# Hybrid decoder layer: keys and values projected between the recurrent branch's channels, queries last

## The chip, the cores and the metric

The kernel runs on one core of a Trainium2 chip. Its engines work side by side and wait for each other through semaphores: PE (matmul; its weight loads are listed as PEld), DVE (elementwise work and scans), ACT (activation functions, casts and copies), POOL (GpSimd) and SP (which here issues most DMAs). The metric is the device time of one execution in microseconds, as the median of the runs.

## The reference, cut to what matters

One decoder layer is computed for a prompt of 2048 tokens, with 16 meta tokens ahead of it, and for 64 sample tokens.

```python
hn = rmsnorm(x, g_mix_pre)
proj = hn @ w_in
q, k, v, xl, gate = jnp.split(proj, [512, 1024, 1536, 2048], axis=-1)
attn = attend(q, k, v)               # stick-breaking, 8 heads of 64
...
xc = conv_b; xc = xc + xpad[:, j:j + T] * conv_w[j]      # j = 0..3
r = sigmoid(xb @ w_gate_a + b_gate_a);  i = sigmoid(xb @ w_gate_x + b_gate_x)
log_a = -8 * softplus(-lru_lambda) * r
h = exp(log_a) * h + sqrt(-expm1(2 * log_a)) * i * xc    # scan over tokens
...
mixed = concat([attn, lru * gelu(gate)]) @ w_out
x = x + rmsnorm(mixed, g_mix_post)
u = relu(rmsnorm(x, g_mlp_pre) @ w_up)
x = x + rmsnorm((u * u) @ w_down, g_mlp_post)
```

In stick-breaking attention a logit block passes two sigmoids, a running product along the keys and a multiplication; the result is transposed and multiplied with the values. Keys, values, the last hidden state and the last convolution inputs are outputs too.

## The kernel before

**Tiles.** The prompt is worked in four tiles of 512 tokens (NSB = 4, index s); tile 0 also carries the meta and the sample tokens, 592 columns in two chunks. Matmuls run on float32 split into a high and a low part in the fp32r format, three products for each (high x high, high x low, low x high). `gemm` computes 128 output channels for all tokens of a tile: 24 matmuls of 512 columns. `gemm_nat` computes 128 tokens by 512 channels in up to four PSUM accumulators. PSUM buffers have three tags: D (4, projections), T (3, logits and transposes), O (1, attention outputs).

**Weights.** A list `seq` holds the weight tiles in the order of use. `w_next` hands out the next one, already split by ACT (L161) and DVE (L162), splits the one behind it and starts the load of the one after that (SP, L152). Two raw and two split buffers each exist.

**Order of work.** PE's order is the order of the program, written by hand. The other engines' order is made by a scheduler when the kernel is built, out of dependencies and its own clock, so an instruction of DVE, ACT, POOL or SP can stand ahead of one that the program has earlier.

**Input projection.** `inproj(s)` runs, for the four channel groups c of the recurrent branch, the x gemm, the convolution (DVE, L508 and L510) and the gate gemm with GeLU (L527 to L530). After the x gemm of group c+1 come the two small gate matmuls of group c (`gates`, L455) with their sigmoids; they are kept in `held` until then. After the x gemm of group 2 `recur((0, 1))` runs the recurrence of groups 0 and 1: tanh, exp and sqrt on ACT (L466, L467, L469), products and a scan on DVE (L472, L473, L481), the product with the gate (L486) and a store to a DRAM tile `md` (L487). Then come four key gemms, each with a cast and split (L545, L546) and stores to `kd`. The gates of group 3 follow the first of them and `recur((2, 3))` the second (`late`). Then comes the value product (`gemm_nat`, evacuated by `v_evac`, stores to `vd`), and last the generator `queries()` with four query gemms; in the last two the next tile is normalised (`prep`) and transposed into `ahi` and `alo` (L264 to L267).

**Attention as side work.** `Work` holds generators that emit attention: first that of the samples, then `attn`, over tiles, heads and key groups. A step of `attn` may hold a logit block S (L706, then `chain`: sigmoids L642 and L643, scan L647 or L650, product L654), a transpose T (L716, evacuated by L727 and L728; for the meta keys by L722 to L724) and a product with the values V (L738, L740); T follows S, and V follows T, by four steps or more. Each gemm calls `tick` with an estimate of its PE time; `tick` adds that times `rate` to a credit and takes steps while the credit lasts. `rate` is RATE0 in the recurrent groups and RATE1 in keys, values and queries (tiles 1 to 3; in tile 0 it is 0). `need(key)` takes steps at once, without matmuls of a projection between them, until that piece of work is done. A tile's attention can start when its `queries()` has ended.

**After the last projection.** For tile 3 one query gemm is run; then `work.need("s")`, the pool `p1` (the projection's buffers) is closed and the pool `pacc` is opened in its memory. `group(0)` calls `work.need(("a", 0))`. Two more query gemms run while `load` brings `md` of tile 0 through the x buffers of `pacc` (L970) and splits it (L966, L967); then come the output projection of tile 0, the last query gemm, a stage of attention and transposes without gemms (`burst`), and the MLP with the rest of the attention and of the output projections between its gemms.

Of the kernel before, what the change touches and what calls it, by code (L numbers as in the profile page):

```python
# [8 lines left out]
F32 = mybir.dt.float32  # L9
# [3 lines left out]
AF = mybir.ActivationFunctionType  # L13
ALU = mybir.AluOpType
PSUM = bass.MemoryType.PSUM

P = 128
# [6 lines left out]
DB = 8  # L24
DS = 8
# [4 lines left out]
G0 = 1.5957691216057308  # L30
G1 = 0.07135481627159986
# [56 lines left out]
def _program(tc, I, O, NSB, NSC):  # L88

    nc = tc.nc  # L90
# [39 lines left out]
    seq = []  # L130
    for s in range(NSB):
        for c in range(4):
            seq.append(I["w_in"][12 + c])
            seq.append(I["w_in"][16 + c])
        seq += [I["w_in"][ct] for ct in range(4, 8)] + [I["w_v"][kp] for kp in range(4)]
        if s < NSB - 1:
            seq += [I["w_in"][ct] for ct in range(4)]
    out_w = [I["w_out"][hf, kp] for hf in range(2) for kp in range(4)]
# [295 lines left out]
    def inproj(s, p1, pa, K, ahi, alo, before_k=None):  # L434
# [53 lines left out]
                if s == 0:  # L488
                    nc.sync.dma_start(msd[:, 4 + c, :], gt[:, NP:N])

        held = None
        for c in range(4):
            outs = gemm(hi_, lo_, chunks, before_k=before_k if c == 0 else None)
            if held is not None:
                gates(*held)
            if c == 2:
                recur((0, 1))
            xp = T(p1, [P, 3 + W], F32, "xp")
            if s == 0:
                nc.gpsimd.memset(xp[:, 0:3], 0.0)  # L500
            else:
                nc.scalar.copy(xp[:, 0:3], K["convc"][:, c, :])
            for (a, b), o in zip(chunks, outs):
                nc.scalar.copy(xp[:, 3 + a:3 + b], o)
            nc.scalar.copy(K["convc"][:, c, :], xp[:, NP:NP + 3])
            cw = K["cw"]
            xc = T(p1, [P, W], F32, "xc", 1)
            nc.vector.tensor_scalar(xc[:, 0:NP], xp[:, 0:NP], cw[:, c, 0:1], K["cb"][:, c:c + 1], op0=ALU.mult, op1=ALU.add)  # L508
            for j in range(1, 4):
                nc.vector.scalar_tensor_tensor(xc[:, 0:NP], xp[:, j:j + NP], cw[:, c, j:j + 1], xc[:, 0:NP],  # L510
                                               op0=ALU.mult, op1=ALU.add)
            if s == 0:
                spad = T(p1, [P, DB, DS + 3], F32, "spad", 2)
                nc.gpsimd.tensor_copy(spad[:, :, 0:3], K["sconv"][:, c])
                nc.gpsimd.tensor_copy(spad[:, :, 3:3 + DS], xp[:, 3 + NP:3 + N].rearrange("p (b t) -> p b t", b=DB))
                nc.gpsimd.tensor_copy(K["csamp"][:, c], spad[:, :, DS:DS + 3])
                xs = xc[:, NP:N].rearrange("p (b t) -> p b t", b=DB)
                nc.vector.tensor_scalar(xs, spad[:, :, 0:DS], cw[:, c, 0:1], K["cb"][:, c:c + 1], op0=ALU.mult, op1=ALU.add)
                for j in range(1, 4):
                    nc.vector.scalar_tensor_tensor(xs, spad[:, :, j:j + DS], cw[:, c, j:j + 1], xs, op0=ALU.mult, op1=ALU.add)  # L520
            outs = gemm(hi_, lo_, chunks)
            g = T(p1, [P, W], F32, "g")
            for (a, b), o in zip(chunks, outs):
                nc.scalar.copy(g[:, a:b], o)
            g = g[:, 0:N]
            gt = T(p1, [P, W], F32, "gt", 2)[:, 0:N]
            nc.vector.scalar_tensor_tensor(gt, g, G1, g, op0=ALU.mult, op1=ALU.mult)  # L527
            nc.vector.scalar_tensor_tensor(gt, gt, G0, g, op0=ALU.add, op1=ALU.mult)
            nc.scalar.activation(gt, gt, AF.Sigmoid)
            nc.vector.tensor_tensor(gt, gt, g, op=ALU.mult)  # L530
            gts.append(gt)
            held = (c, xc)

        late = lambda c: gates(*held) if c == 0 else recur((2, 3)) if c == 1 else None


        work.rate = RATE1 if s else 0.0
        for c in range(4):
            outs = gemm(hi_, lo_, chunks)
            late(c)  # L540
            kf, hi, lo = stage("sf", F32), stage("sh", F32R), stage("sl", F32R)
            for (a, b), o in zip(chunks, outs):
                nc.scalar.copy(kf[:, a:b], o)
# [16 lines left out]
        def v_evac(t, o):  # L560
# [19 lines left out]
            else:  # L580
# [4 lines left out]
        gemm_nat(lambda k, t: ahi[:, k, t * P:min(t * P + P, N)], lambda k, t: alo[:, k, t * P:min(t * P + P, N)],  # L585
                 5 if s == 0 else 4, None, v_evac)

        def queries():
            ys = None
            for c in range(4):  # L590
# [3 lines left out]
                if c == 3 and s + 1 < NSB:  # L594
                    def nxt(k):
                        if k > 0:
                            xpose_k(ys, k - 1, K["g_pre"], ahi[:, k - 1], alo[:, k - 1])
                outs = gemm(hi_, lo_, chunks, after_k=nxt)
                if nxt is not None:
                    nxt(KC)  # L600
                hi, lo = stage("sh", F32R), stage("sl", F32R)
# [583 lines left out]


    next(queries)
    work.need("s")
    close(p1)
    pacc = xpool[0] = pool("pacc")  # L1190
# [149 lines left out]
```

## Time and profile before

| What | Value |
| --- | --- |
| median of 3 runs | 2724.7 us (2722.91 to 2725.73) |
| profiled execution | 2732.83 us, span 2731.0 us |
| granted PE clock, mean | 0.992 |
| busy DVE, ACT, POOL | 67%, 53%, 13% |
| input projection of tile 3, without queries | 478 to 596 us |
| first query gemm of tile 3 | from 596 us |
| output projection of tile 0 | from 627 us |

A row of the timeline has the start, the duration, engine, line, operation, output and inputs, shapes, the count, and in brackets the engine's idle time before it and what ended it. A row of the list of waits has the total, the number of times and the longest. Matmuls are pipelined and their ends are modelled: the start of one to the start of the next tells what each costs.

### The profile page before, as it was taken

What the parts mean: (1) busy time and instruction counts of PE and PEld (TensorE: products, weight loads), DVE (VectorE), ACT (ScalarE), POOL (GpSimd) and SP (SyncE); (2) the same over time, 40 slices, a digit from 0 to 9 for tenths busy, and PEclk for the clock granted to TensorE, in tenths of its full rate; (3) what the DMA queues carried; (4) which work ended last, traced back from release to release, by engine and by line L of the source; (5) the groups of instructions that cost most, each with busy time, mean ns of one, the idle gap of its engine ahead of it and who ended that gap; (6) DMA issues with size and microseconds to landing.
All of it is one profiled execution on the core that took longest, in us unless ns stands there. A gap on an engine that the chain in (4) does not pass through costs nothing.

```text
span 2731.0 us, 36901 instructions
## 1 busy us (share of the span) xinstructions
PE 2672.5 (98%) x13804; PEld 2213.0 (81%) x13804; DVE 1839.0 (67%) x2898; ACT 1453.2 (53%) x2430; POOL 352.9 (13%) x579
## 2 busy tenths in 40 slices
PE   8999999999899999999999999999999999999997
PEld 7987768778688888878888888878888887898895
DVE  6556377876877777869777777786777746333344
ACT  6556376865666554546565555565555534332232
POOL 3122331111211101011100100110000001000002
PEclk9999999999899999999999999999999999999999
DMA  4466858485444433445343334443333244222223
GB/s 164 137 216 194 260 179 233 123 229 167 144 128 119 115 110 103 140 145 176 100 115 112 101 112 125 161 149 110 101 102 101 76 162 160 82 81 85 78 85 108
DMA packets 149155, 368.11 MB, mean 135 GB/s; under 512 B 20992, under 2 KB 51200, under 8 KB 148976
## 3 DMA queue, kind: packets, MB, share of 16 engines
q1 hardware_dynamic: 103792, 287.35, 32.3%
q0 software_dynamic: 45184, 78.41, 11.6%
q8 instruction: 109, 1.79, 0.3%
q14 instruction: 70, 0.57, 0.1%
HBM read 305.51 MB, written 60.04 MB: 134 GB/s over the span
## 4 chain that ended last, share of the span: by engine, by line
PE 88%; DVE 6%; issue 2%; DMA 1%; ACT 1%; POOL 1%; SPq 0%; POOLq 0%; DVEq 0%; ACTq 0%
PE D L184 13%; PE D L186 13%; PE D L185 13%; PE D L216 11%; PE D L217 11%; PE D L218 11%; PE T L716 5%; PE T L706 4%; PE O L738 2%; PE O L740 2%; PE D L455 1%; DVE wlo L162 1%; POOL rstd L240 1%; PE O L222 1%; PE O L221 1%
## 5 line engine op out<-in xcount | busy, mean ns | idle before, releaser
L162 DVE TENSOR_TENSOR wlo<-wraw,whi 128x1024 fp32r<-128x1024 f32 x368 | 453.1, 1231 | 453.7 <-ACT whi L161 443.4
L184 PE MATMUL D<-ahi,whi 128*128 128x512 f32 (+3 forms) x1920 | 709.3, 369 | 0.0
L186 PE MATMUL D<-ahi,wlo 128*128 128x512 f32 (+3 forms) x1920 | 685.6, 357 | 0.2 <-DVE wlo L162 0.2
L185 PE MATMUL D<-alo,whi 128*128 128x512 f32 (+3 forms) x1920 | 684.0, 356 | 1.3 <-DVE ms L236 1.3
L161 ACT CAST whi<-wraw 128x1024 fp32r<-128x1024 f32 x368 | 386.9, 1051 | 493.5 <-PE D L217 300.1
L216 PE MATMUL D<-whi,uh 128*128 128x512 f32 x1024 | 417.5, 408 | 5.1 <-DVE y L1020 4.9
L184 PEld LDWEIGHTS D<-ahi,whi 128*128 128x128 f32 x1920 | 364.5, 190 | 50.1 <-issue 7.3
L217 PE MATMUL D<-whi,ul 128*128 128x512 f32 x1024 | 405.0, 396 | 0.0
L186 PEld LDWEIGHTS D<-ahi,wlo 128*128 128x128 f32 x1920 | 364.3, 190 | 50.0 <-DVE wlo L162 0.6
L218 PE MATMUL D<-wlo,uh 128*128 128x512 f32 x1024 | 404.5, 395 | 0.0
L185 PEld LDWEIGHTS D<-alo,whi 128*128 128x128 f32 x1920 | 365.2, 190 | 42.7 <-issue 1.7
L642 ACT ACTIVATE keep<-T,nbias 128x512 f32<-128x512 f32 (+6 forms) x352 | 210.1, 597 | 250.1 <-PE T L706 242.4
L650 DVE TENSOR_TENSOR_SCAN pb<-keep,carry 128x513 f32<-128x513 f32 (+1 forms) x228 | 267.5, 1173 | 74.9 <-ACT keep L642 71.8
L728 DVE TENSOR_TENSOR wtl<-T,wth 128x512 fp32r<-128x512 f32 (+1 forms) x320 | 191.2, 602 | 83.8 <-ACT wth L727 83.3
L727 ACT CAST wth<-T 128x512 fp32r<-128x512 f32 (+1 forms) x320 | 166.6, 523 | 129.5 <-PE T L716 128.9
L216 PEld LDWEIGHTS D<-whi,uh 128*128 128x128 f32 x1024 | 192.8, 188 | 46.6 <-DVE y L1020 6.6
L218 PEld LDWEIGHTS D<-wlo,uh 128*128 128x128 f32 x1024 | 192.6, 188 | 46.6
L217 PEld LDWEIGHTS D<-whi,ul 128*128 128x128 f32 x1024 | 193.3, 189 | 38.7
L643 ACT ACTIVATE beta<-T,bias 128x512 f32<-128x512 f32 (+6 forms) x352 | 208.4, 592 | 0.0
L654 DVE TENSOR_TENSOR beta<-beta,pb 128x512 f32<-128x512 f32 (+7 forms) x360 | 202.8, 563 | 0.0
L716 PE MATMUL T<-ident,beta 128*128 128x128 f32 (+1 forms) x1216 | 193.1, 276 | 7.2 <-DVE ms L236 3.6
L706 PE MATMUL T<-kv,q 128*128 128x512 f32 (+5 forms) x640 | 178.5, 361 | 4.1 <-DVE alo L267 3.3
(235 smaller groups left out, 3472.1 us busy)
## 6 DMA issues: line engine op xcount, KB each, us to landing
wraw<-in_w_up SPq DMA_DIRECT2D x128, 512.0 KB
wraw<-in_w_down SPq DMA_DIRECT2D x128, 512.0 KB
wraw<-in_w_in SPq DMA_DIRECT2D x64, 512.0 KB
q<-qd POOLq DMA_DIRECT2D x64, 256.0 KB, 4.9
wraw<-in_w_out SPq DMA_DIRECT2D x32, 512.0 KB
kv<-kd POOLq DMA_DIRECT2D x48, 256.0 KB
kv<-vd POOLq DMA_DIRECT2D x48, 256.0 KB, 4.1
y<-in_x_prompt SPq DMA_DIRECT2D x16, 512.0 KB
```

Source lines behind the costliest of these rows:

```text
L161: nc.scalar.copy(hi, r)
L162: nc.vector.tensor_tensor(lo, r, hi.bitcast(F32), op=ALU.subtract)
L184: nc.tensor.matmul(o, whi[:, k, :], ahi(k, a, b), start=(k == 0), stop=False)
L185: nc.tensor.matmul(o, whi[:, k, :], alo(k, a, b), start=False, stop=False)
L186: nc.tensor.matmul(o, wlo[:, k, :], ahi(k, a, b), start=False, stop=(k == KC - 1))
L216: nc.tensor.matmul(o, h, whi[:, kk, :], start=st, stop=False)
L217: nc.tensor.matmul(o, l, whi[:, kk, :], start=False, stop=False)
L218: nc.tensor.matmul(o, h, wlo[:, kk, :], start=False, stop=sp)
L642: nc.scalar.activation(keep[:, o:512], S, AF.Sigmoid, bias=nbias, scale=-0.125)
L650: nc.vector.tensor_tensor_scan(pb[:, o:513][:, ::-1], kr, kr, 1.0 if carry is None else carry, op0=ALU.mult, op1=ALU.bypass)
L706: nc.tensor.matmul(o, H["q"][:, e, i * P:(i + 1) * P], kap, start=(e == 0), stop=(e == 1))
L716: nc.tensor.transpose(t[0:kn, i * P:(i + 1) * P], w[:, c0:c0 + kn], ident)
```

## The change

Keys and values move between the recurrent groups. The order in a tile is now: key gemm 0, values, x and gate gemm 0; key gemm 1, x and gate gemm 1; key gemm 2, x and gate gemm 2; x and gate gemm 3; key gemm 3; then the four query gemms. `held` becomes a list: the gates of a group are run after the next gemm that asks for them, now a key gemm for groups 0, 1 and 3 and the x gemm 3 for group 2. `recur((0, 1))` stays behind x gemm 2. `recur((2, 3))` moves behind the first query gemm. RATE0, which now holds for all but key gemm 3 and the queries, goes from 0.2 to 0.35; RATE1 stays 0.5. For tile 3 `lru_outputs` (the stores of the last state) moves behind the first query gemm.

```diff
 for s in range(NSB):
     for c in range(4):
-        seq.append(I["w_in"][12 + c])
-        seq.append(I["w_in"][16 + c])
-    seq += [I["w_in"][ct] for ct in range(4, 8)] + [I["w_v"][kp] for kp in range(4)]
+        seq += [I["w_in"][4 + c]] if c < 3 else []
+        seq += [I["w_v"][kp] for kp in range(4)] if c == 0 else []
+        seq += [I["w_in"][12 + c], I["w_in"][16 + c]]
+    seq.append(I["w_in"][7])
...
-        held = None
+        held = []
+        def keys_of(c):
+            outs = gemm(hi_, lo_, chunks, before_k=before_k if c == 0 else None)
+            if held:
+                gates(*held.pop())
...
+        def values():
+            gemm_nat(lambda k, t: ahi[:, k, t * P:min(t * P + P, N)], lambda k, t: alo[:, k, t * P:min(t * P + P, N)],
+                     5 if s == 0 else 4, None, v_evac)
         for c in range(4):
-            outs = gemm(hi_, lo_, chunks, before_k=before_k if c == 0 else None)
-            if held is not None:
-                gates(*held)
+            if c < 3:
+                keys_of(c)
+            if c == 0:
+                values()
+            outs = gemm(hi_, lo_, chunks)
+            if held:
+                gates(*held.pop())
             if c == 2:
                 recur((0, 1))
...
-            held = (c, xc)
-        late = lambda c: gates(*held) if c == 0 else recur((2, 3)) if c == 1 else None
+            held.append((c, xc))
         work.rate = RATE1 if s else 0.0
-        for c in range(4):
-            outs = gemm(hi_, lo_, chunks)
-            late(c)
...
+        keys_of(3)
...
                 outs = gemm(hi_, lo_, chunks, after_k=nxt)
+                if c == 0:
+                    recur((2, 3))
...
             for _ in queries:
                 pass
-        lru_outputs(s, K)
+            lru_outputs(s, K)
...
     next(queries)
+    lru_outputs(NSB - 1, K)
     work.need("s")
...
-RATE0, RATE1, RATE2, RATE3, RATE4, BURST = 0.2, 0.5, 0.5, 0.55, 0.3, 4.0
+RATE0, RATE1, RATE2, RATE3, RATE4, BURST = 0.35, 0.5, 0.5, 0.55, 0.3, 4.0
```

The bodies of `keys_of` and `values` (with `v_store` and `v_evac`) are those of the old loops, unchanged.

More of the change, by code (lines that the diff above doesn't have):

```diff
@@ L489, in recur @@
                     nc.sync.dma_start(msd[:, 4 + c, :], gt[:, NP:N])
-        held = None
-        for c in range(4):
+        held = []
+        def keys_of(c):
             outs = gemm(hi_, lo_, chunks, before_k=before_k if c == 0 else None)
-            if held is not None:
-                gates(*held)
[L496 to L520, printed above, removed]
-            outs = gemm(hi_, lo_, chunks)
[L522 to L531, printed above, removed]
-            held = (c, xc)
@@ L534, in inproj @@
-        late = lambda c: gates(*held) if c == 0 else recur((2, 3)) if c == 1 else None
-        work.rate = RATE1 if s else 0.0
-        for c in range(4):
-            outs = gemm(hi_, lo_, chunks)
-            late(c)
+            if held:
+                gates(*held.pop())
             kf, hi, lo = stage("sf", F32), stage("sh", F32R), stage("sl", F32R)
@@ L588, in queries @@
+        work.rate = RATE1 if s else 0.0
+        keys_of(3)
         def queries():
```

39 lines of the change are left out of this document (37 added, 2 removed).

## Prediction

> **What bounds the kernel now.** I read the page first (engine shares, chain of waits), then the waits of the matrix engine (PE), then busy time by stage, and last the timeline of the one stage that stands out.
>
> ```profile
> span 2731.0 us, 36901 instructions
> PE 2672.5 (98%) x13804; PEld 2213.0 (81%) x13804; DVE 1839.0 (67%) x2898; ACT 1453.2 (53%) x2430; POOL 352.9 (13%) x579
> PE 88%; DVE 6%; issue 2%; DMA 1%; ACT 1%; POOL 1%; SPq 0%; POOLq 0%; DVEq 0%; ACTq 0%
> ```
>
> PE is busy 98% of the span, and the chain of waits is PE for 88%. The change removes no matmul, so it can only remove PE's idle time, 2731.0 - 2672.5 = 58.5 us in all, and time at a reduced clock. Where is it? First PE's waits from 176 to 602 us, the input projections of tiles 1 to 3, which are what the change reorders:
>
> ```profile
> PE T L706 <- DVE alo L267: 0.6, 1, 0.6
> ...
> PE D L186 <- DVE wlo L162: 0.2, 1, 0.2
> ```
>
> These are the first and last of five rows, each of 0.2 to 0.6 us, about 1.7 us together. Then the stages (columns: length, busy time and instruction count of PE, weight loads, DVE, ACT, POOL, granted clock, DMA share, GB/s):
>
> ```profile
> 478.00:602.00 124.00, 123.33 (x585) 99.34 (x584) 98.97 (x177) 92.51 (x161) 19.64 (x40) 1.00 0.58 167
> 602.00:614.00 12.00, 6.06 (x26) 4.36 (x25) 10.34 (x19) 7.19 (x15) 2.16 (x4) 0.83 0.93 263
> 614.00:627.00 13.00, 13.00 (x54) 10.47 (x54) 7.74 (x10) 6.82 (x11) 0.00 (x0) 0.90 0.78 269
> 687.00:719.00 32.00, 19.49 (x95) 14.99 (x94) 29.89 (x57) 22.37 (x43) 7.71 (x14) 0.79 0.56 172
> ```
>
> Tile 3's projection (478 to 602) keeps PE full. Evening out DVE and ACT inside it can therefore win next to nothing. Two stages lose time: 602 to 614 (5.94 us idle) and 687 to 719 (12.5 us idle, but DVE is busy 29.89 of 32: bound by DVE, and the change moves none of its work). So the question is what becomes of 602 to 614.
>
> **The stage from 602 to 614.** PE's timeline:
>
> ```profile
> 602.33 0.39 PE L738 MATMUL O<-wth,kv 128*128 128x512 f32 x1
> ...
> 602.80 0.27 PE L716 MATMUL T<-ident,beta 128*128 128x128 f32 x1
> ...
> 603.67 0.72 PE L706 MATMUL T<-kv,q 128*128 128x512 f32 x2 [0.25 <-DVE wtl L728]
> ...
> 607.26 0.33 PE L740 MATMUL O<-wtl,kvt 128*128 128x128 f32 x1 [1.35 <-DVE wtl L728]
> 611.59 0.76 PE L738 MATMUL O<-wth,kv 128*128 128x512 f32 x1 [4.00 <-DMA kvt<-vd]
> ...
> 613.52 0.78 PE L184 MATMUL D<-ahi,whi 128*128 128x512 f32 x1
> ```
>
> After the first query gemm of tile 3 the program calls work.need(("a", 0)): the attention of tile 0 must end before its output projection is set up. What is left of it is emitted with no gemm between the steps, so each V product (L738, L740) waits for its weights to come through ACT and DVE. The 4.00 us before 611.59 are put down to a DMA, but that product reads wth, and DVE wrote it last, behind other work:
>
> ```profile
> 608.92 1.20 DVE L162 TENSOR_TENSOR wlo<-wraw,whi 128x1024 fp32r<-128x1024 f32 x1
> ...
> 610.81 0.68 DVE L724 TENSOR_TENSOR wth<-T,wth 16x512 fp32r<-16x512 f32 x1
> ```
>
> 610.81 + 0.68 = 611.49, just ahead of 611.59. The clock pays too: 0.83 over 12 us and 0.90 over 13 us are 4.1 + 2.6 = 6.7 us at half clock, ending near 616.6; PE works from 611.59, so it loses half of 5.0 us, 2.5 us. The flush costs 5.9 + 2.5 = **8.4 us**.
>
> **Part 1: the planner's credit.** A gemm ticks 5.12 us (3 x 1.92 less 0.64), the value product 16 x 1.28 = 20.5, a gate pair 1.5. Before, one tile has 8 gemms and three gate pairs at 0.2 (45.5 x 0.2 = 9.1) and 8 gemms, values and a gate pair at 0.5 (62.9 x 0.5 = 31.5): 40.6. After: 11 gemms, values, three gate pairs at 0.35 (81.3 x 0.35 = 28.5) and 5 gemms and a gate pair at 0.5 (13.6): 42.0. Tile 3 has one query gemm ahead of the flush, so 32.9 against 34.3. Over tiles 1 to 3 that is 114.0 against 118.4: **4.3 more**. I walked the planner's rule step by step with both orders. Before, 45 logit blocks (S) and 37 V steps are out when the flush begins, 46 and 40 when it ends, for 2.5 of credit. After, 47 and 40: tile 0's last head ends during that query gemm and the flush is empty. The trace bears out the first walk, by its counts of L706, two for each S,
>
> ```profile
> 0.00:602.45 602.45, 19.04 (x88) 16.03 (x88) 1.00 0.63 191
> 602.45:613.50 11.05, 1.59 (x4) 0.96 (x4) 0.84 0.96 271
> ```
>
> and of V steps (L738):
>
> ```profile
> 0.00:602.45 602.45, 12.50 (x36) 6.78 (x36) 1.00 0.63 191
> 602.45:613.50 11.05, 2.16 (x5) 0.85 (x4) 0.84 0.96 271
> ```
>
> (88 + 4) / 2 = 46 S; 36 + 5, less one that stands on the border, 40 V. So term 1 is -8.4 us.
>
> **Part 2: the new hand-over.** The same place gets a new last piece of work. The recurrence of channel groups 2 and 3 moves from the second key gemm to the first query gemm, and the pool p1, in whose memory the x buffers of the output projection lie, closes right behind. Today's hand-over:
>
> ```profile
> 605.89 0.37 SPq L558 DMA_DIRECT2D vd<-vst  x1
> ...
> 610.05 0.33 SPq L1170 DMA_DIRECT2D g_mix_post<-in_g_mix_post  x1
> 610.44 0.42 SPq L970 DMA_DIRECT2D x<-md  x1
> ...
> 616.39 1.05 ACT L966 CAST ahi<-x 128x1024 fp32r<-128x1024 f32 x1 [1.72 <-DMA x<-md]
> ...
> 617.47 1.23 DVE L967 TENSOR_TENSOR alo<-x,ahi 128x1024 fp32r<-128x1024 f32 x1 [1.41 <-ACT ahi L966]
> ...
> 626.89 0.39 PE L216 MATMUL D<-whi,ahi 128*128 128x512 f32 x1
> ```
>
> The last value store is issued at 605.89; SP's next free buffer comes at 610.05, 4.2 us later. From there to the first operand ready (618.70) are 8.65 us, and PE needs it at 626.89: 8.2 us of slack. What the moved recurrence takes is seen where it runs today:
>
> ```profile
> 541.76 1.88 PE L455 MATMUL D<-xc,gw 128*128 128x512 f32 x4
> ...
> 543.13 0.72 ACT L456 ACTIVATE ii<-D,params 128x512 f32<-128x512 f32 x1
> ...
> 545.76 0.77 ACT L466 ACTIVATE b<-r,c 128x512 f32<-128x512 f32 x1
> ...
> 556.06 0.68 DVE L486 TENSOR_TENSOR gt<-ii,gt 128x512 f32<-128x512 f32 x1
> ```
>
> Gates to gated output: 541.76 to 556.74, 15.0 us. ACT starts it while the next gemm runs, ahead of its place in the program, and I take it that it does so again. Counted from the gates of group 3: 15.0 + 4.2 (store landed) + 8.65 (load and split) = 27.9 us. PE meanwhile does the gates (1.9) and three query gemms. The last two took 13.4 us from 613.52 to 626.89, 1.6 of it lost to the clock: 11.8. The walk gives them one S, three T and three V more, at under 0.5 each (a V takes 602.80 - 602.33 = 0.47): 15.2. The first, by the same prices, is 5.4 and two S, T and V each: 7.8, an estimate. In all 24.9. So PE waits **3 us** at the output projection. Bounds: 0 if the recurrence takes 3 us less or the x buffers lie on tiles that come free earlier; 9 if it starts only after the query gemm. SP issues in order: a load of x that waits would hold the following w_out load, which is wanted a quarter of the half, over 5 us, later, and hides.
>
> Would so short a stall cost clock? Two others, of 1.6 and 2.1 us:
>
> ```profile
> 1220.00:1224.00 4.00, 2.38 (x11) 1.63 (x10) 2.94 (x7) 3.09 (x8) 2.10 (x3) 1.00 0.91 317
> 1224.00:1230.00 6.00, 6.00 (x28) 4.84 (x27) 5.59 (x9) 3.00 (x5) 3.85 (x3) 1.00 0.92 307
> ...
> 2266.00:2272.00 6.00, 3.86 (x17) 2.69 (x16) 5.33 (x10) 4.51 (x9) 2.50 (x3) 1.00 0.46 145
> 2272.00:2276.00 4.00, 4.00 (x11) 2.85 (x9) 3.56 (x6) 1.84 (x4) 2.10 (x3) 0.57 0.88 287
> ```
>
> The first leaves the clock at 1.00; the second is followed by 4 x 0.43 x 2 = 3.4 us at half, a loss of 1.7. At 3 us I count half of that, +0.8. The Trainium skill (TensorE: Matmul & The Clock Gate, Part 1: The HAM clock gate) says that the clock halves after an idle window of about 3.4 us; the trace shows it after 2.1, so the measurement decides, and by the page this term would be nothing.
>
> **Part 3: queries.** Into each tile's query stage come two recurrences on DVE. Its rows, and the query stage of tile 2:
>
> ```profile
> L481 DVE TENSOR_TENSOR_SCAN ii<-r,hcar,b 128x512 f32<-128x512 f32 x4 | 5.1, 1282 | 0.1
> ...
> L472 DVE SCALAR_TENSOR_TENSOR b<-r,b 128x512 f32<-128x512 f32 x4 | 2.8, 690 | 3.0 <-ACT b L469 3.0
> ...
> L473 DVE TENSOR_TENSOR b<-b,ii 128x512 f32<-128x512 f32 x4 | 2.7, 686 | 0.1
> ...
> L486 DVE TENSOR_TENSOR gt<-ii,gt 128x512 f32<-128x512 f32 x4 | 2.7, 684 | 0.0
> ```
>
> ```profile
> 445.00:479.00 34.00, 33.21 (x179) 27.20 (x178) 27.22 (x51) 22.27 (x43) 5.39 (x11) 1.00 0.85 245
> ```
>
> One channel group is 1.28 + 0.69 + 0.69 + 0.68 = 3.3 us, two 6.7. DVE has 34 - 27.2 = 6.8 us free there: full to the brim if both fall there, well off if group 2 runs early. The next tile's transposed operand leaves DVE at the end of this stage. I take +1 us (0 to 4). In the key, value and recurrent gemms the work is the same and more even: 0, or -1.7 at best. The second DVE-bound stage gets 7 V and 7 transposes for 9 and 8: 0, or -2. SP issues the same transfers in another order; a tile's 28 key and value stores, some 0.4 us each (605.89), stand between weight loads that run a gemm ahead, as today: 0.
>
> **Sum:** -8.4 + 3 + 0.8 + 1 = **-3.6 us**. It is made against the profiled execution (2732.8 us, span 2731.0); the median of the three runs is 2724.7, 8.1 lower, and I carry the difference over: 2721.
>
> **Rivals.**
> A (forecast, 0.45): flush gone, half given back at the hand-over: 2721, own range 2717 to 2725.
> B (0.38), the hand-over hides: the x buffers lie on early tiles, or group 3 ends a few us sooner. Then -8.4, with up to -2 in the DVE-bound stage: 2715. For it: the 8.2 us of slack today. Against it: 27.9 against 24.9.
> C (0.12), slower: the recurrence isn't run ahead. It then starts with the query gemm's end: 11.0 (545.76 to 556.74) + 4.2 + 8.65 = 23.9 against 15.2, 9 us of stall with 2.5 of clock loss, as at the flush, and DVE is full in the query stages of tiles 1 and 2 (+4 each): -8.4 + 9 + 2.5 + 8 = +11, or 2732 to 2736. It decides on the sign once the hand-over stall and the queries together pass 8.4 us.
> D (0.05): the credit isn't what ends attention early, and a flush remains: 2725.
> The Trainium skill (TensorE: Matmul & The Clock Gate, Architectural detail) has ACT and DVE as strict FIFO queues; the L724 row above agrees, and it is what makes C cost so much.
>
> **How the numbers follow.** 0.2% is 5.4 us, about what a measurement of this kernel can tell from no change. Faster (under 2719.3): 0.12 from A, 0.31 from B: 0.43. Slower (over 2730.1): 0.11 from C. The rest, 0.46, lies within. The range, 2711 to 2730, leaves out most of C and the tail of B.
>
> **What would show it.** Right: no stage near 602 with PE half idle; the last L738 of tile 0 inside a gemm; DVE's L486 of group 3 a few us after the first query gemm and x<-md behind it; a wait of the first output-projection matmul on x or ahi. Wrong: a flush of V products without gemms; x loaded as early as today (B); long waits on alo L267 ahead of a tile's first key gemm (C).

## The result and the profile after

| | before | after |
| --- | --- | --- |
| median of 6 runs | 2724.5 us (2722.7 to 2725.7) | 2743.0 us (2740.1 to 2747.1) |
| ratio to before, 95% interval | | 1.0067 (1.0057 to 1.0077) |
| profiled execution | 2732.8 us, span 2731.0 | 2741.5 us, span 2739.7 |
| a second profile of before | 2725.3 us, span 2723.5 | |

The change makes the kernel slower by 18.5 us; 2721, within 0.2%, was predicted. Of the 8.1 us between the first profile of before and its median, 6.0 were an odd start: in that execution the projection of tile 0 took 176.6 us, in a second profile of the same kernel 170.6. Tiles 1 and 2 differ by at most 0.7 us between these two profiles. From here on "before" is this second profile. The page of after, its span, busy times and chain of waits:

```profile
span 2739.7 us, 36914 instructions
...
PE 2669.3 (97%) x13804; PEld 2207.8 (81%) x13804; DVE 1835.4 (67%) x2898; ACT 1455.8 (53%) x2433; POOL 351.9 (13%) x579
...
PE 89%; DVE 5%; ACT 3%; DMA 1%; issue 1%; POOL 1%; SPq 0%; DVEq 0%; POOLq 0%; ACTq 0%
```

Nothing stands out there: same PE instructions, same shares. The loss has to be looked for stage by stage. I cut both traces at the first matmul of a gemm (in the changed kernel a tile starts with key gemm 0, in the old one with x gemm 0) and took the lengths:

| Stage, us | before | after | difference |
| --- | --- | --- | --- |
| tile 0 | 170.6 | 170.5 | -0.1 |
| tile 1 | 152.1 | 152.8 | +0.7 |
| tile 2 | 150.6 | 164.7 | **+14.1** |
| tile 3 up to its queries | 117.3 | 122.2 | **+4.9** |
| query gemm 0, with the flush of before | 17.2 | 8.7 | **-8.5** |
| query gemms 1 and 2, to the output projection | 12.6 | 18.7 | **+6.1** |
| output projection of tile 0 | 53.7 | 55.2 | +1.5 |
| query gemm 3 and the attention behind it | 38.6 | 37.4 | -1.2 |
| MLP and the rest, to the end | 2010.6 | 2009.6 | -1.0 |

The flush went as forecast. The loss is in tiles 2 and 3, which the prediction had priced at nothing. Tile 2 as a row of the busy times by stage, before and then after (columns: length, busy time and count of PE, weight loads, DVE, ACT, POOL, granted clock, DMA share, GB/s):

```profile
322.70:473.30 150.60, 149.01 (x819) 113.01 (x817) 109.43 (x188) 102.67 (x180) 38.02 (x59) 1.00 0.69 212
```

```profile
323.30:488.00 164.70, 154.62 (x829) 117.88 (x826) 113.27 (x200) 108.66 (x193) 37.22 (x62) 0.97 0.67 192
```

PE idles 164.70 - 154.62 = 10.1 us instead of 1.6 (+8.5), and is busy 5.6 us longer: 10 more matmuls and a clock of 0.97. No engine's total has grown by much, so it is a wait, not an overload. PE's waits in tile 2, all of before and then those of after that are over half a us together:

```profile
PE T L706 <- DVE alo L267: 0.6, 1, 0.6
PE O L895 <- DMA kv<-in_cache_v,ix: 0.5, 1, 0.5
PE T L716 <- ACT beta L643: 0.4, 1, 0.4
```

```profile
PE O L751 <- DVE wtl L739: 4.9, 1, 4.9
PE T L727 <- ACT beta L654: 3.7, 2, 1.9
PE T L265 <- ACT beta L654: 1.1, 1, 1.1
```

The first is a wait of attention's V product. In the others a transpose waits for a PSUM buffer of tag T, which the sigmoid that makes beta is the last to read: L727 is attention's, and L265 is the next tile's, which takes no beta at all. What stands in front of the largest? ACT's timeline of after:

```profile
408.15 0.64 ACT L738 CAST wth<-T 128x512 fp32r<-128x512 f32 x1
408.81 1.28 ACT L468 ACT_TABLE_LOAD   x1
410.11 0.72 ACT L468 ACTIVATE r<-r,cm 128x512 f32<-128x512 f32 x1
410.83 1.28 ACT L470 ACT_TABLE_LOAD   x1
412.13 0.63 ACT L470 ACTIVATE b<-b 128x512 f32<-128x512 f32 x1
412.67 0.57 ACT L564 COPY xp<-D 128x512 f32<-128x512 f32 x1
413.13 1.05 ACT L162 CAST whi<-wraw 128x1024 fp32r<-128x1024 f32 x1
...
414.17 0.92 ACT L738 CAST wth<-T 128x384 fp32r<-128x384 f32 x3
```

and DVE's:

```profile
412.79 0.69 DVE L473 SCALAR_TENSOR_TENSOR b<-r,b 128x512 f32<-128x512 f32 x1 [2.63 <-ACT b L470]
...
415.12 1.28 DVE L482 TENSOR_TENSOR_SCAN ii<-r,hcar,b 128x512 f32<-128x512 f32 x1
...
418.28 1.22 DVE L163 TENSOR_TENSOR wlo<-wraw,whi 128x1024 fp32r<-128x1024 f32 x1
419.42 1.08 DVE L739 TENSOR_TENSOR wtl<-T,wth 128x384 fp32r<-128x384 f32 x3
```

and PE's:

```profile
414.81 0.34 PE L749 MATMUL O<-wth,kv 128*128 128x384 f32 x1
420.03 0.69 PE L751 MATMUL O<-wtl,kv 128*128 128x384 f32 x1 [4.88 <-DVE wtl L739]
```

The recurrence of group 1 (exp L468, sqrt L470) holds ACT from 408.81 to 412.7, each function with a table load of 1.28 us ahead of it. For 2.63 us DVE has nothing, then everything at once: recurrence, convolution (left out above), a weight split, and only at 419.42 the low part that PE has wanted since it issued the high product at 414.81. Blocks like this one stand in front of the two waits on beta at L727 too: tanh, exp and sqrt of the next group, and the load for attention's sigmoids behind them, hold ACT from 433.52 to 439.54, and those of the last group from 453.14 to 459.73, with one copy between. Why did this not happen before? The square roots of tile 2's four recurrences, and the first logits of the prompt's attention, with the first and last start (before, then after):

```profile
L469 ACT ACT_TABLE_LOAD  x4: 1283/1283/1283, 349.2 to 391.9; - x4
```

```profile
L706 PE MATMUL T<-kvt,q x4: 218/248/278, 403.3 to 413.1; 128*128 128x128 f32 x4
```

```profile
L470 ACT ACT_TABLE_LOAD  x4: 1283/1283/1283, 385.2 to 455.9; - x4
```

```profile
L717 PE MATMUL T<-kvt,q x4: 225/250/275, 385.0 to 398.0; 128*128 128x128 f32 x4
```

Before, the last square root of tile 2 was over at 393 and the prompt's attention began at 403: there they never met. Now the recurrences are spread to 457, since keys and values stand between the groups, and attention begins at 385, since more credit falls into the tile's first gemms and the samples' share is done sooner.

Meeting alone isn't a loss, however. In tile 3 of before all four recurrences (table loads from 495.7 to 548) ran beside the prompt's attention, with the same blocks on ACT, one of them from 524.10 to 530.09, and PE waited 0.7 us in all. Here are the logits whose sigmoids stood behind that block, the second sigmoid, and the transpose that takes over the logits' PSUM buffer (there are three of tag T; a transpose and another logit block take the other two); then the same for the block of tile 2 in after that ends at 439.54:

```profile
527.32 0.34 PE L706 MATMUL T<-kv,q 128*128 128x144 f32 x2
...
530.38 0.37 ACT L643 ACTIVATE beta<-T,bias 128x144 f32<-128x144 f32 x1
...
531.60 0.38 PE L716 MATMUL T<-ident,beta 128*128 128x128 f32 x2
```

```profile
436.00 0.34 PE L717 MATMUL T<-kv,q 128*128 128x144 f32 x2
...
439.83 0.37 ACT L654 ACTIVATE beta<-T,bias 128x144 f32<-128x144 f32 x1
...
440.26 0.44 PE L727 MATMUL T<-ident,beta 128*128 128x128 f32 x2 [1.93 <-ACT beta L654]
```

Before, PE came to the transpose 4.3 us after the logits, and the sigmoid had left their buffer 0.8 us earlier. After, it came 2.3 us after them (440.26 - 1.93 - 436.00) and had to wait 1.9. So such a block costs PE time only where attention's next step comes before ACT is through with it. Of the 2.8 us between these two cases 2.0 are the closer steps; the rest is that the logits came earlier in the block. Whether a fourth buffer of tag T would hide it wasn't tried.

### The profile page after: what moved, and what is told of

Read it like the earlier page. It is cut to its first block, busy times and chain, and to the rows that moved or that the text cites. A ratio compares the mean times of both kernels' runs of the same rounds, so it can differ in the third digit from the quotient of the medians.

```text
span 2739.7 us, 36914 instructions
## 1 busy us (share of the span) xinstructions
PE 2669.3 (97%) x13804; PEld 2207.8 (81%) x13804; DVE 1835.4 (67%) x2898; ACT 1455.8 (53%) x2433; POOL 351.9 (13%) x579
## 4 chain that ended last, share of the span: by engine, by line
PE 89%; DVE 5%; ACT 3%; DMA 1%; issue 1%; POOL 1%; SPq 0%; DVEq 0%; POOLq 0%; ACTq 0%
PE D L185 13%; PE D L187 12%; PE D L186 12%; PE D L217 11%; PE D L218 11%; PE D L219 11%; PE T L727 5%; PE T L717 4%; PE O L749 2%; PE O L751 2%; DVE wlo L163 1%; PE D L456 1%; PE O L223 1%; PE O L222 1%; POOL rstd L241 1%
## 5 line engine op out<-in xcount | busy, mean ns | idle before, releaser
L727 PE MATMUL T<-ident,beta 128*128 128x128 f32 (+1 forms) x1216 | 192.7, 276 | 9.2 <-ACT beta L654 4.4
```

The source lines that it names most:

```text
L727: nc.tensor.transpose(t[0:kn, i * P:(i + 1) * P], w[:, c0:c0 + kn], ident)
```

## The experiments

**before_again: the kernel before, profiled once more.** No edit.

> The kernel before once more, for a second profile: its first profiled execution was 8.1 us over the median of its timed runs. If that execution was typical of profiled ones, this span is again about 2731 and the stage from 602 to 614 looks the same; if it was an odd one, the span is about 2723 and the missing 8 us lie in some stage (I expect the flush and the stage behind it, with the half clock).

Span 2723.5 us; tile 0 took 170.6 us, the other stages much as in the first profile, the flush too. The first profile was the odd one. This one is the yardstick above.

**rate_only: the old order with the new credit.**

```diff
-        work.rate = RATE1 if s else 0.0
         for c in range(4):
...
+        work.rate = RATE1 if s else 0.0
         def queries():
...
-RATE0, RATE1, RATE2, RATE3, RATE4, BURST = 0.2, 0.5, 0.5, 0.55, 0.3, 4.0
+RATE0, RATE1, RATE2, RATE3, RATE4, BURST = 0.35, 0.5, 0.5, 0.55, 0.3, 4.0
```

> The old order with the one rate of 0.35 through recurrent groups, keys and values, and 0.5 in the queries: the credit over tiles 1 to 3 is about that of before (41.0 a tile against 40.6). Theory R (the loss of 18.5 us comes from running attention at 0.35 between the recurrent gemms, where its transposes and V products wait on ACT and DVE behind the recurrence): 2735 to 2743, with PE waits of several us on wtl or beta in tile 2. Theory O (the loss comes from the order, that is from the recurrence of groups 2 and 3 behind the first query gemm and the hand-over to the output projection): 2722 to 2727.

2729.1 us (10 runs) against 2725.7; ratio 1.0012 (1.0002 to 1.0021): between the ranges of the two theories. Tile 2 took 153.3 us, 2.7 more. Its attention also began early, at 386.6, but only the last of its four square roots, at 400, came after that. In tile 3, where before had no such wait, PE now came to such a transpose 3.0 us after the logits and waited 2.8 us for their buffer, with exp and two table loads on ACT in front. So the credit alone, by setting the steps closer, can make this stall in the old order.

**order_kind: the new order with the old rates by kind of gemm** (0.2 beside x and gate gemms, 0.5 beside keys, values, queries).

```diff
             if c < 3:
+                work.rate = RATE1 if s else 0.0
                 keys_of(c)
             if c == 0:
                 values()
+            work.rate = RATE0 if s else 0.0
...
-RATE0, RATE1, RATE2, RATE3, RATE4, BURST = 0.35, 0.5, 0.5, 0.55, 0.3, 4.0
+RATE0, RATE1, RATE2, RATE3, RATE4, BURST = 0.2, 0.5, 0.5, 0.55, 0.3, 4.0
```

> The new order with the old rates by kind of gemm: 0.5 at keys, values and queries, 0.2 at x and gate gemms (credit 41.5 a tile). Theory R: the long waits in tile 2 go, the hand-over wait of about 3 us stays and the flush is empty or nearly so: 2720 to 2728. Theory O: as slow as the changed kernel, 2738 to 2745.

2734.2 us (7 runs); 1.0029 (1.0018 to 1.0041): again between the theories. Tile 2: 159.3 us, 8.7 more than before. So neither part alone makes the 14.1: credit 2.7, order 8.7, both 14.1. The waits in tile 2 are other ones here, most of them for split weights (4.7 us for low parts, 1.1 for a high one). In front of the longest, 2.75 us to 424.62, it is DVE that is busy: a scan (1.28 us) and a gating (0.68) of a recurrence stand, with attention and convolution, between the cast of the high part and the low part at 423.35, while ACT idles for 1.97 us. So a recurrence can hold up PE through DVE as well.

**before_r53: the old order, the flush emptied by credit alone.**

```diff
-RATE0, RATE1, RATE2, RATE3, RATE4, BURST = 0.2, 0.5, 0.5, 0.55, 0.3, 4.0
+RATE0, RATE1, RATE2, RATE3, RATE4, BURST = 0.2, 0.53, 0.5, 0.55, 0.3, 4.0
```

> The old order with RATE1 at 0.53 for 0.5: by the planner's rule 47 logit blocks and 40 V steps are out at the hand-over, as in the changed kernel, so the flush is empty, and nothing else of the change is there. Term 1 of the prediction (the flush costs 8.4 us): 2716 to 2718. If the flush costs little in the typical run (the profiled run before was 8 us over the median): 2722 to 2726.

2721.3 us (10 runs) against 2725.7; 0.9983 (0.9974 to 0.9993): between the two cases. The flush is gone: 17.2 fell to 7.3 us. But the two query gemms behind it went from 12.6 to 22.1, and nearly all of that gain with them. What the kernel gains stands elsewhere: in this profile tiles 1 and 2 are 3.7 us longer and everything from query gemm 3 on is 7.8 shorter. ACT's timeline there:

```profile
609.89 0.59 ACT L603 CAST sh<-D 128x512 fp32r<-128x512 f32 x1
617.12 1.04 ACT L966 CAST ahi<-x 128x1024 fp32r<-128x1024 f32 x1 [6.64 <-DMA x<-md]
619.75 1.04 ACT L966 CAST ahi<-x 128x1024 fp32r<-128x1024 f32 x1 [1.59 <-DMA x<-md]
620.70 1.55 ACT L727 CAST wth<-T 128x512 fp32r<-128x512 f32 x3
```

and PE's longest wait from 600 to 626:

```profile
PE O L738 <- ACT wth L727: 4.1, 1, 4.1
```

The casts of x stand ahead of attention's casts in ACT's queue and wait for their load, issued at 608.83. Three casts that PE needs come out together at 620.70. The flush had been covering that load; without it the load's time, some 8 us, is what PE sees next.

**r53_yload: the same, with tile 0's x loaded into other, already free buffers.**

```diff
-                    t = T(xpool[0], shape, F32, "x", 2)
+                    if self.s == 0:
+                        t = T(xp_, [P, DM], F32, "y", 4).rearrange("p (k n) -> p k n", k=2)
+                    else:
+                        t = T(xpool[0], shape, F32, "x", 2)
```

> The old order with RATE1 at 0.53, where the flush is empty but half of what it cost came back as a wait behind the load of x on ACT (the cast of x, L966, waits for its transfer and the casts of attention stand behind it). Here the first output projection's input is loaded into the y buffers, which are free in tile 3, so that the transfer need not wait until p1 is closed. If that transfer is what holds ACT: the 4.1 us wait in front of L738 goes and the time is 2714 to 2718. If something else holds ACT: 2720 to 2723 as without it.

2721.2 us (10 runs); 0.9987 (0.9978 to 0.9997): the longest wait fell from 4.1 to 2.7 us, the two gemms stayed at 22.1. A load of x still held ACT: it idled 3.84 us ahead of the cast at 618.19, for a load issued from 607.4 on. So the load's own time seems to hold it rather than the buffers; freeing them earlier wins nothing that can be measured.

**after_split: the changed kernel, the recurrences one group at a time.**

```diff
-            if c == 2:
-                recur((0, 1))
+            if c:
+                recur((c - 1,))
...
-                    recur((2, 3))
+                    recur((3,))
```

> The changed kernel with the recurrence run one channel group at a time, each behind the gemm that follows its gates, instead of in pairs. Theory B (the waits in tile 2 come from the block of two recurrences, which stands on ACT and DVE ahead of attention's casts and products): the longest waits in tile 2 fall under 2 us and the time to 2728 to 2735. Theory R (attention at 0.35 overloads DVE and ACT there, whatever the order of the recurrences; and each group alone needs its own ACT table loads): no gain, 2740 to 2748.

2743.8 us (4 runs); 1.0073 (1.0048 to 1.0097). No gain: tile 2 at 163.6 us with the same 4.9 us wait. The edit changed little of what ran there: the scheduler had spread the recurrences of tile 2 already (their square roots' loads start from 385.2 to 455.9 in the changed kernel and from 384.7 to 454.3 here). So pairs of groups that come at once aren't the cause. The wait on x at the output projection was 5.9 us here.

**after_early: the changed kernel, the last recurrences back behind the last key gemm.**

```diff
         keys_of(3)
+        recur((2, 3))
...
-                if c == 0:
-                    recur((2, 3))
```

> The changed kernel with the recurrence of groups 2 and 3 written right behind the last key gemm, ahead of the first query gemm, with PE's order unchanged. If the late place of that recurrence costs the hand-over (3 us of wait and the clock behind it) and the waits in the query stage of tile 2: 2732 to 2737. If the place in the program is of no account because the scheduler runs it as soon as its gates are there: 2741 to 2745, and the hand-over wait stays.

2736.6 us (7 runs); 1.0050 (1.0036 to 1.0064), 6.4 us under the changed kernel's 2743.0, or 4.6 by the two ratios, whose intervals just overlap. The wait on x at the output projection is gone and the two query gemms take 15.7 us instead of 18.7. The output projection, in whose start the last of that wait and the half clock behind it fell, is 2.6 us shorter. But query gemm 0 takes 11.5 instead of 8.7, with a wait of 2.6 us on beta. By the profiles the late place cost 3.0 + 2.6 - 2.8 = 2.8 us in all; the rest of their difference is elsewhere, 2.0 of it in tile 0. Tile 2 keeps its waits, 4.9 us for wtl and 4.0 for beta.

**after_vrate: the credit moved into the value product** (0.2 elsewhere up to key gemm 3).

```diff
             if c == 0:
+                work.rate = 0.8 if s else 0.0
                 values()
+                work.rate = RATE0 if s else 0.0
...
-RATE0, RATE1, RATE2, RATE3, RATE4, BURST = 0.35, 0.5, 0.5, 0.55, 0.3, 4.0
+RATE0, RATE1, RATE2, RATE3, RATE4, BURST = 0.2, 0.5, 0.5, 0.55, 0.3, 4.0
```

> The changed order with 0.2 at the key, x and gate gemms and 0.8 at the values, for the same credit: 47 logit blocks and 40 V steps at the hand-over as in the changed kernel, but fewer of them beside a recurrence (in tile 2, 10 logit blocks for 16 between the first x gemm and the last key gemm). Theory R: most of the 10 us of waits in tile 2 go, 2727 to 2733. If the waits come from the order alone: 2739 to 2745.

2745.5 us (4 runs); 1.0086 (1.0057 to 1.0116). Against theory R, the time didn't fall. Tile 2 fell to 159.6 us, but tile 1 rose from 152.8 to 159.6: PE waits there for the samples' keys (kv<-in_cache_k, 3.4 us) and for a beta of theirs (1.4). Sparing one place has loaded another. The wait on x is 5.4 us, but it is 4.4 to 5.1 in three kernels below that leave tile 3 as it is, so this edit need not be its cause.

**before_no2 and after_no2: both orders with no attention in tile 2 up to its queries.** The same edit in each:

```diff
-        work.rate = RATE0 if s else 0.0
+        work.rate = RATE0 if s % 2 else 0.0
...
-        work.rate = RATE1 if s else 0.0
+        work.rate = RATE1 if s % 2 else 0.0
...
         def queries():
+            work.rate = RATE1 if s else 0.0
```

> The kernel before with the planner's rate at 0 through tile 2's projection up to its query gemms (0.5 there); the attention left out of tile 2 comes later, in tile 3 and in a longer flush. Read for one thing, the length of tile 2's stage without attention beside its recurrent, key and value gemms. Both theories: 150.6 us less the attention products that go, about 125 to 132 us. It is the yardstick for the next kernel; its total means nothing.

> The changed kernel with the same rates as the run before it: no attention beside tile 2's recurrent, key and value gemms. Theory M (attention and the recurrence of groups 0 and 1 meet on ACT and DVE): tile 2 is as long as in the kernel before with the same rates, within 2 us. Theory O (the new order of gemms costs by itself, through late weight splits): tile 2 stays 8 us or more longer than there.

Tile 2 of the old order, then of the new:

```profile
322.80:451.30 128.50, 128.25 (x629) 98.59 (x628) 77.03 (x108) 78.47 (x118) 14.97 (x18) 1.00 0.64 203
```

```profile
323.30:453.60 130.30, 128.95 (x645) 99.14 (x644) 78.25 (x110) 82.49 (x122) 12.52 (x14) 1.00 0.59 192
```

128.5 and 130.3 us: the new order by itself costs 1.8 us, as theory M had it. The other 12.3 of the 14.1 appear only with attention beside it.

**after_norec2 and norec2_all: the changed kernel without recurrences in tile 2.** First those of groups 0 and 1:

```diff
         def recur(cs):
+            if s == 2 and cs == (0, 1):
+                for c in cs:
+                    nc.sync.dma_start(md[s][:, 4 + c, :], gts[c][:, o0:o0 + SB])
+                return
```

> The changed kernel with the recurrence of channel groups 0 and 1 of tile 2 left out (tanh, exp, sqrt, two multiplies, scan, gating; the ungated halves are stored). Planner and order unchanged. Theory M: the 4.9 us wait for wtl and the clock lost behind it go, tile 2 falls from 164.7 to 152 to 156 us and the total by about as much. Theory O: tile 2 stays at 162 us or more, since the weight splits and the attention stand where they stood.

Tile 2 took 157.1 us, 7.6 less and just above theory M's range. The total says nothing here (2742.6 us in one run, with a tile 0 of 176.2 us again). PE's waits of over half a us in tile 2:

```profile
PE T L731 <- ACT beta L658: 3.7, 2, 1.9
PE T L265 <- ACT beta L658: 1.1, 1, 1.1
```

The 4.9 us for wtl are gone, those on beta not. Then all four (the condition is `s == 2` alone):

> The changed kernel with all four recurrences of tile 2 left out (the ungated halves are stored). With those of groups 0 and 1 out, tile 2 was still 157.1 us against 150.6 before. Theory M (the rest is the recurrences of groups 2 and 3 beside attention): the waits on beta fall under 1 us and tile 2 comes to 150 to 154 us. Rival (the rest is attention beside the convolution and the gates): the waits on beta stay at 4 us and tile 2 at 156 us or more.

```profile
325.40:476.90 151.50, 150.02 (x828) 115.25 (x826) 102.14 (x181) 86.19 (x169) 36.92 (x62) 1.00 0.70 209
```

151.5 us, 0.9 more than before the change. Of the waits only 1.1 and 0.4 us are left. All but this 0.9 us of tile 2's loss hangs on the recurrences.

**noact2: only the recurrences' work on ACT left out in tile 2.**

```diff
-            for c in cs:
+            for c in cs if s != 2 else ():
                 nc.scalar.activation(bs[c], rs[c], AF.Tanh, scale=K["c4"][:, c:c + 1])
                 nc.scalar.activation(rs[c], rs[c], AF.Exp, scale=K["cm8"][:, c:c + 1])
-            for c in cs:
+            for c in cs if s != 2 else ():
                 nc.scalar.activation(bs[c], bs[c], AF.Sqrt)
...
-                nc.vector.scalar_tensor_tensor(b_, a_, 1.0, b_, op0=ALU.add, op1=ALU.mult)
+                nc.vector.scalar_tensor_tensor(b_, a_, 1.0, a_ if s == 2 else b_, op0=ALU.add, op1=ALU.mult)
```

> The changed kernel with only the recurrences' work on ACT left out in tile 2 (tanh, exp, sqrt and the table loads they bring); the products, the scan and the gating stay on DVE, from other numbers. Theory ACT (the table loads hold attention's sigmoids and casts, and let the recurrence reach DVE late): the 4.9 us wait and the waits on beta go, and tile 2 is as short as with all four recurrences out, within 2 us. Theory DVE (the recurrence's 3.3 us per group in DVE's queue ahead of the low part): the 4.9 us wait stays at 3 us or more, and tile 2 over 158 us.

```profile
324.70:476.20 151.50, 150.01 (x829) 115.15 (x827) 113.03 (x200) 85.90 (x169) 37.21 (x62) 1.00 0.72 209
```

151.5 us again, with DVE's work all there (113.03 us in 200 instructions, against 113.27 in 200). ACT has 85.90 us instead of 108.66: 22.8 us less for four recurrences, 5.7 each. The table loads of tile 2 in the changed kernel,

```profile
L653 ACT ACT_TABLE_LOAD x5 | 6.4, 1283 | 0.1
L468 ACT ACT_TABLE_LOAD x4 | 5.1, 1283 | 0.1
L470 ACT ACT_TABLE_LOAD x4 | 5.1, 1283 | 0.0
```

are 13 and here 1. So without the recurrences' work on ACT, 5.7 us a group and two thirds of it table loads, PE's waits in tile 2 fall to 1.1 and 0.4 us, and the recurrence's 3.3 us a group on DVE alone cost nothing. Whether they add to the stall once ACT has delayed them isn't tested: in the rows above a scan and a gating stand on DVE ahead of the low part. In this run the total was 2731.1 us, 10 less than the changed kernel's profiled execution; tile 2 alone is 13.2 shorter, but the wait on x at the output projection is 5.1 us here instead of 2.4.

**early_poolpow and r53_poolpow: the square root taken to POOL,** with the whole computation kept, in after_early and in before_r53.

```diff
-                nc.scalar.activation(bs[c], bs[c], AF.Sqrt)
+                nc.gpsimd.tensor_tensor(bs[c], bs[c], half[:, 0:1].to_broadcast([P, N]), op=ALU.pow)
```

> The changed kernel with recur((2, 3)) behind the last key gemm, and the recurrence's square root taken from ACT to POOL (a power of one half): per recurrence one table load of 1.28 us and 0.63 us of function leave ACT. If ACT's table loads are what PE waits for in tile 2, its waits shrink: tile 2 from 163.6 to 155 to 160 us, the total 3 to 8 us below the 2736.6 of the same kernel with the root on ACT. If the other load (exp) is enough to keep the wait, or POOL's power is slower than the 3.2 us it replaces (table load twice, function), no gain: 2736 or more.

> The old order with RATE1 at 0.53 and the same square root on POOL. There the recurrence meets little attention (tile 2 has 1.5 us of PE waits), so by the same theory it wins next to nothing: 2719 to 2723 against 2721.3. If it gains more than 4 us, ACT's table loads cost in places that the waits do not show; if it loses, POOL's power is slow and delays the gates.

4046 and 4029 us (4 runs each). One row of early_poolpow's groups, kept apart by shape, says why:

```profile
L472 POOL TENSOR_TENSOR b<-b,half 128x512 f32<-128x512 f32 x12 | 984.2, 82018 | 86.0 <-ACT b L469 66.3 <-DMA out_k_prompt<-sf 14.4 <-ACT convc L567 5.3
```

82 us for each power. I had guessed at a few us from the 0.73 us that the powers of the norms, one column each, take on average. Whether a lighter ACT would give the time back with the whole computation kept stays untested.

**kind_early: order_kind with the last recurrences behind the last key gemm,** to see whether the two mends add up. The edit is that of after_early.

> The new order with attention at 0.2 through the recurrent gemms and 0.5 through keys, values and queries, and the recurrence of groups 2 and 3 right behind the last key gemm. If the two costs of the change (attention that meets the recurrence, a late hand-over) add up, each is mended by its own edit: about 2727 to 2729 us. If they are one cost, no better than the better of the two alone: 2734. If the new order is worth something once both are mended: under 2719.

2735.7 us (6 runs); 1.0035 (1.0022 to 1.0048): no better than order_kind's 2734.2. The scheduler had run that recurrence early in order_kind already (its square root starts at 610.15 us there, at 611.28 here, 619.86 in the changed kernel), so the edit moved nothing, and it doesn't test whether the two costs add up. The waits on ahi and alo at the output projection are 2.3 us in both. They may still be the recurrence's: in both the load of x is issued 3.5 us behind the store of the last gated half (md<-gt at 615.95, x at 619.45 in order_kind).

Best of all: the old order with RATE1 at 0.53, 0.17% under before (interval 0.07% to 0.26%). No version of the new order came under the old.

## Why the prediction was wrong, point by point

**Term 1, the flush, -8.4: right.** The stage fell by 8.5 us; the planner's walk had it right that the credit empties it. before_r53 shows the limit of reading this as a gain: there too the flush went (-9.9) and came back in the two query gemms behind it (+9.5), with casts that waited for x.

**Part 2, the hand-over, 3 us of wait: right in mechanism, near in size by luck.** The chain in after, rows of SP, then ACT, then PE:

```profile
625.19 0.38 SPq L488 DMA_DIRECT2D md<-gt  x1
...
628.03 0.82 SPq L981 DMA_DIRECT2D x<-md  x2
```

```profile
636.41 1.04 ACT L977 CAST ahi<-x 128x1024 fp32r<-128x1024 f32 x1 [2.76 <-DMA x<-md]
```

```profile
637.51 0.50 PE L217 MATMUL D<-whi,ahi 128*128 128x512 f32 x1 [2.41 <-ACT ahi L977]
...
638.77 0.50 PE L218 MATMUL D<-whi,alo 128*128 128x512 f32 x1 [0.76 <-DVE alo L978]
```

2.41 + 0.76 = 3.2 us. The store of the last gated half landed at 628.02, and the load of x was issued at 628.03. But the terms were off and cancelled: from the gates of group 3 (608.23) to the first operand (638.72) it took 30.5 us instead of 27.9, and PE came to the output projection (635.10) after 26.9 instead of 24.9. In three kernels that leave tile 3 as it is (after_norec2, norec2_all, noact2) the wait on ahi alone was 4.4, 4.9 and 5.1 us. The clock behind it was mis-sized: at half for 3.4 us from 640, a loss of 1.7 where 0.8 was counted as half a chance of it. Of the stage's +6.1, 2.4 is the wait on ahi, 1.3 two shorter waits, and 2.2 more PE work, mostly attention that was moved here: 14.82 us against 12.60.

**Part 3, queries, +1: nothing came.** The four query gemms of tile 2 took 34.7 us, 34.6 before. DVE didn't fill.

**Part 3, the step that failed: "In the key, value and recurrent gemms the work is the same and more even: 0, or -1.7 at best."** Measured: +14.1 in tile 2 and +4.9 in tile 3. Three things were left out.
- The bound had no upper side. -1.7 came from the waits of the old order. In its tile 2 recurrence and attention did not meet; in its tile 3 they met, but with attention's steps far enough apart. That they would meet in the new tile 2, with more credit beside them, could be read from the two orders and the rates; no row of before shows the price.
- Only DVE was priced, at 3.3 us for each group. What tile 2 can't do without is ACT's part: tanh, exp and sqrt with table loads, 5.7 us a group, in blocks of 4 to 6 us. Such blocks were in the trace of before, in tile 3 even right in front of attention's sigmoids, and PE waited for none of them.
- The work in sum stayed much the same (ACT 102.7 and 108.7 us in tile 2, a share of 68 and 66%), which is what "more even" looked at. The share didn't show the loss: it is the lower one in the slower stage. What showed it was the time from logits to the transpose that takes over their PSUM buffer, 4.3 us in the old tile 3 and 2.3 in the new tile 2, with a block of 6 us on ACT around it.

That the loss in tile 2 needs ACT's part is shown (noact2: 164.7 to 151.5 us), and that it needs attention beside it (order alone 1.8 us); DVE's part alone makes none of it. That the spacing of the steps decides where a block costs is read from the rows and from rate_only; no run changed the spacing alone in the new order without moving steps elsewhere. In tile 3 no run left anything out. PE's longest wait there, and the stage around it:

```profile
PE D L187 <- DVE wlo L163: 2.3, 1, 2.3
```

```profile
582.00:592.00 10.00, 7.98 (x32) 6.70 (x33) 8.72 (x15) 2.84 (x8) 3.31 (x7) 0.83 0.55 170
```

A low weight part was late, behind a recurrence and steps of attention on DVE, and 10 x 0.17 x 2 = 3.4 us at half clock followed. Which of the two engines began it there stays open.

**The DVE-bound stage, 0 or -2:** -1.2. **The start from the median:** right; 6.0 of the first profile's 8.1 us were an odd tile 0.

**The rivals.** C, the slower one, named 2732 to 2736, but by another mechanism: a recurrence that is not run ahead, and DVE full in the query stages. The first was half true: tanh of group 3 ran at 613.62, in the middle of the first query gemm, but exp at 617.84, 1 us before that gemm's end, and sqrt at 619.86, behind it. The second was wrong: the queries of tile 2 kept their length. B fell with the 3.2 us at the hand-over. What happened, a recurrence in one queue with steps of attention that stand close, was not among the rivals, and so the range stopped at 2730.

## What to carry to other kernels

When a reorder interleaves two chains that were apart, list for each engine the longest unbroken block that either chain puts in its queue, table loads included. Ask which work that another engine waits for can land behind it, and compare the block with the time until that work is wanted; shares of busy time don't show this. A stall that you remove may be covering a load: look for what is issued inside it and when that lands. And where two parts of a change act on each other, price the corners: in tile 2 the credit alone cost 2.7 us, the order alone (with the old rates) 8.7, the order with no attention beside it 1.8, and both 14.1.

## What the runs showed of the hardware

- Exp, sqrt and sigmoid each bring a table load of 1283 ns on ACT when they alternate. The Trainium skill (ScalarE: Activation LUTs, What ACT_TABLE_LOAD costs) gives the same 1283 ns and adds a drain, 2.66 us in all for a switch. The rows above don't show the drain: cast from 408.15 for 0.64, load from 408.81, exp from 410.11, 1.30 us from the load's start to the function's.
- A power on POOL takes 82 us for 128x512 (early_poolpow), 160 ns a column, while for one column (L241 of after) it takes 0.54 to 1.67 us, 0.55 in the median.
- In the traces here the clock is granted in full or at half: from 441.6 to 445 in after it is 0.51, and matmuls of 512 columns start 0.43 us apart (442.15 and 442.58) where they take 0.23 soon after (446.16 and 446.39). The wait of 2.3 us in tile 3 was followed by 3.4 us at half clock, the one of 4.9 us in tile 2 by twice that:

```profile
410.00:425.00 15.00, 10.12 (x41) 7.83 (x40) 12.28 (x22) 10.13 (x18) 1.03 (x2) 0.77 0.37 110
```

15 x 0.23 x 2 = 6.9 us. PE worked through the last 4.6 of these (from 420 to 425 the clock is 0.54: 5 x 0.46 x 2), so the 4.9 us stall cost about 2.3 more. The length of a wait doesn't decide by itself: the one of 1.9 us at 440.26 was followed by those 3.4 us at half clock, while rate_only's waits of 2.5 and 2.8 us at 406.12 and 537.00 left the clock at 1.00.
